# Sixth and seventh product of region (0, 2) in quarters, with measures moved

## The chip, the cores and the metric

The kernel runs on one core of a Trainium2 chip. A core has a matrix engine, TensorE (PE in the profile; PEld is its loading of weights), VectorE (DVE), ScalarE (ACT), GpSimd (POOL) and SyncE (SP). Here POOL and SP mostly issue transfers between HBM and the core's memory. Each engine works through its own queue in order; a wait of one instruction holds up all that stand behind it on the same engine.

The metric is the time of one execution on the device, in microseconds. Before the change it is 1515.66 us, the median of three runs.

## The reference

```python
x = np.matmul(a, b)                       # a, b: 4096 x 4096, float32
return np.where(x > 0, x, alpha * x)      # alpha = 0.01
```

A square matrix product of 4096, and a leaky ReLU on it. The inputs are normally distributed.

## The kernel before, in words

**Arithmetic.** The matmuls run in float16 with sums in float32. The product is formed with Winograd's variant of Strassen's scheme, with 7 products in place of 8, in two levels. The output is cut into 4 x 4 regions of 1024 x 1024, named (g, j) by row group and column group. On the upper level a region takes, for each of two halves of the inner dimension's pairing, blocks A11, A12, A21, A22 and B11, B12, B21, B22; PRODUCTS (L669) lists the seven products:

```python
PRODUCTS = [("a11", 0, 0), ("a12", 1, 0), ("s2", 0, 0), ("s3", 0, 1), ("s1", 0, 0), ("a22", 1, 0), ("s4", 1, 1)]
```

The first is a11 B11, the second a12 B21, and then follow s2 T2, s3 T3, s1 T1, a22 T4 and s4 B22. The letters s are sums of A's blocks, T sums of B's. VectorE makes the T sums in place over the tiles of B: first t3 = B22 - B12, then t2 = B11 + t3, then T4 and T1 (all at the line of b_sum, L606). The sums of A are made once for a row group.

A product as a whole is 64 matmuls of 128 x 512 (L929). It can be done "in quarters", that is with the scheme applied a second time: 7 quarter products of 16 matmuls of 128 x 256 (L773), 112 in all. That needs quarter sums of both operands (sums_of_a, L709 to L728; sums_of_b, L697 to L707), which VectorE makes as well, and additions of the quarter results. Sums of A in quarters are kept in HBM (kept_q) by the first region that makes them, and loaded by those after it.

**Order.** (0, 0) is done within the start, while A and B arrive. Then come (0, 1), (0, 2), (0, 3), then (1, 2), (1, 0), (1, 3), (1, 1), and so on in the four row groups. The order of instructions on each engine is written out by hand (a manual schedule), with no planner: the program's text is the queue of each engine. The flags in_quarters, first_of_group, second_of_group, in_fourth, turning (the last region of a row group) and by_steps (the last region of row group 0) choose the form of each region. Before the change, only regions of row groups 1 to 3 that aren't the last of their group do products in quarters (beside the set FIRST, which does its first product so); row group 0 does all seven as whole products.

**Around a region.** The first product goes to four banks of the accumulator memory, y. ScalarE copies them to the other four, z (L1336), since the second product adds to z, and the third to y. Results leave the accumulators by copies on ScalarE (L952) or additions on VectorE, get the leaky ReLU on VectorE (L328) and are stored by SP (L1258). Tiles of B have two buffers for each of four names. So a tile for the next region can be fetched (POOL at L564, or SP at L561 for halves that have been kept in float16) only when the last product that reads the tile before it is done. In quarters, the first half of a tile comes free earlier or later by the order ks, (0, 1) or (1, 0), in which the two halves are taken.

**T1 in parts.** Where the fourth and fifth products are in quarters, T1's second half is made in four steps of half a tile's columns (L1445): two that make T4 and two that make T1. They stand on VectorE behind the T sums, the leaky ReLU of u1 and two whole sums.

**Measures.** The kernel measures the magnitude of its inputs, to be able to say at its end that float16 with sums of sums was accurate, or else take another path. A measure of a block of A or B is four squares on ScalarE (L235), three additions and a fold on VectorE (L244 to L290). MeasureInTwo does with two buffers, so its third and fourth square (L263) each wait for an addition (L261). Tables say which block is measured in which region and at which place: EARLY begins it ahead of the region's first product and ends it right behind it or, for some, after the T sums ("afterwards"); MEASURED has those in the middle and later; IN_C is a region whose measure takes its room from the buffers of the outputs. A measure has to read a tile of B before a sum overwrites it.

In (0, 3), the squares, the four copies to z and t3 are interleaved (by_steps):

```python
if by_steps:
    for k in ks:
        b_sum(B(0, 1, k), B(1, 1, k), B(0, 1, k), SUB)
        if k == ks[0]:
            next(ends_of_early)
for m in [] if by_steps else at_once:
    m.end()
if not in_first:
    for mt in range(MT):
        nc.scalar.copy(z[mt], y[mt])
```

Of the kernel before, what the change touches and what calls it, by code (L numbers as in the profile page):

```python
# [31 lines left out]
MT = 4  # L32
# [19 lines left out]
def kernel(  # L52
# [167 lines left out]
    class Measure:  # L220
# [21 lines left out]
        def end(self):  # L242
            total, *more = self.held[:3]
            nc.vector.tensor_add(total, total, more[0])  # L244
            if len(self.held) == 3:
                self.square(3)
            nc.vector.tensor_add(total, total, more[1])
            nc.vector.tensor_add(total, total, self.held[3])
            fold(self.which, total, self.place(2), self.pairs)

    class MeasureInTwo(Measure):
# [15 lines left out]

        def end(self):
            for _ in self.parts_of_end():
                pass  # L270
# [206 lines left out]
    for i in range(1, len(steps) - last_turn):  # L477
        t, h, u, first, last = steps[i]
        head = 0 if not new[i] else KC // 2 if last else KC
        groups = [([(mt, c) for c in range(head) for mt in range(MT)], None)]  # L480
        if i == 4:

            groups[0][0].sort(key=lambda x: (x[1] // 2, x[0] == MT - 1))
        if i == 1:
            head = KC // RUNS[u]
            groups = [([(mt, c) for mt in range(MT) for c in range(head)], None)]
        groups += [([(mt, c) for c in range(head, KC)], mt if last else None) for mt in range(MT)]
        following = turns[i + 1] if i + 1 < len(steps) else []
        where = [0, 3] if len(following) < 4 else range(4)
        if i > 1 and i + 1 < len(steps):  # L490
            for fetch in fetches[i + 1]:
                fetch()
        if i == 5:

            for u, nt in ((u, nt) for u in range(2) for nt in range(2)):
                for c in range(0, KC, 4):
                    load_b(1, u, c, 4, nt)
        t, h, u, first, last = steps[i]
        if first:
            banks = {(mt, nt): new_bank(2 * mt + nt) for mt in range(MT) for nt in range(2)}  # L500
            if h not in part:
                part[h] = x_pool.tile([P, MT, 2 * NT], FP32, name="part", tag="x")
        for g, (todo, leaves) in enumerate(groups):
            for mt, c in todo:
                for nt in range(2):
                    mm(banks[mt, nt], h, u, mt, nt, c, first and c == 0, last and c == KC - 1)
            if i == 5 and 1 < g < MT:
                spill(t, h, leaves, banks)
            for piece, turn in enumerate(following):
                if where[piece] == g:  # L510
                    turn()
            if leaves is not None and (i != 5 or g == 1):
                spill(t, h, leaves, banks)
            if leaves is not None and t and i != 5:
                leave_first(h, leaves)
        if i == 3:
            for m in first_columns:
                m.begin()
        if i == 4:
            for m in first_columns:  # L520
                m.end()
            q = quarters_of_first(0)
            f = lambda n: t_of_b21[n].rearrange("p (c n) -> p c n", n=HALF)
            nc.vector.tensor_tensor(f(3), q[1, 1], q[0, 1], SUB)
            nc.vector.tensor_tensor(f(2), f(3), q[0, 0], ADD)
            nc.vector.tensor_tensor(f(4), q[1, 0], f(2), SUB)
# [104 lines left out]
    def judge(line):  # L631
# [26 lines left out]
    A11, A12, A22 = (0, 0, 0), (0, 0, 1), (0, 1, 1)  # L658
# [50 lines left out]
    def sums_of_a(g, name, room, ahead_of_4=None, some=(1, 2, 3, 4), made=None):  # L709
# [5 lines left out]
        def make(n, x0, x1, op):  # L715
# [5 lines left out]
            nc.sync.dma_start(kept_q[name][n - 1], made[n])  # L721
# [162 lines left out]
    for i, (g, j) in enumerate(regions):  # L884

        ks = (1, 0) if in_quarters else (0, 1)
        late_s2 = in_quarters
# [169 lines left out]
        def sixth_in_quarters(pairs, banks, v_pairs, v, y, tq, sq):  # L1057
# [17 lines left out]

            quarter_product(x[0, 0], b[0, 0], into(chain), True)
# [30 lines left out]
        def seventh_in_quarters(y, one, other, tq, sq, between):  # L1107
# [10 lines left out]
            quarter_product(sx(4), b[1, 1], onto(y, 0, 1))  # L1118
# [13 lines left out]
            next(between)  # L1132
            add_pieces(pairs, y)
# [126 lines left out]
        if i == 0:  # L1260
# [6 lines left out]
            first_measure = Measure(0, halves(at[0, 1, 0]) + halves(at[0, 1, 1]), True)  # L1267
# [37 lines left out]
        early = [measure(i, *block, Measure if g else MeasureInTwo) for block in EARLY.get((g, j), [])]  # L1305
        have_t2 = g > KEPT_T.get(j, G)
        by_steps = turning and not g
        at_once, afterwards = ([], early) if in_first or have_t2 else (early[:1], early[1:])
        if by_steps:
            ends_of_early = at_once[0].parts_of_end()  # L1310
# [12 lines left out]
        if (g, j) == LATE:  # L1323
            fetch_b(i, [(1, 1)], ks)
        if second_of_group:
            sums_of_s3(g, (2,))
        if by_steps:
            for k in ks:
                b_sum(B(0, 1, k), B(1, 1, k), B(0, 1, k), SUB)
                if k == ks[0]:  # L1330
                    next(ends_of_early)
        for m in [] if by_steps else at_once:
            m.end()
        if not in_first:
            for mt in range(MT):
                nc.scalar.copy(z[mt], y[mt])  # L1336
        if have_t2:
# [3 lines left out]
        in_c = (g, j) == IN_C  # L1341
        if in_c:
            m = measure(i, *B22)
            m.room = [c_pool.tile([P, 2048], BF16, name="sq", tag=f"c{n}") for n in (side, side, 1 - side, 1 - side)]
            for n in range(4):
                m.square(n)
        if second_of_group:
# [8 lines left out]
        if by_steps:  # L1356
            for k in ks:
                next(ends_of_early)
                b_sum(B(0, 0, k), B(0, 1, k), B(0, 0, k), ADD)
            next(ends_of_early)  # L1360
        for k in [] if by_steps else ks:
            if have_t2:
                if late_s2:
                    load_s2(g, ks[1], True)
                break
            b_sum(B(0, 1, k), B(1, 1, k), B(0, 1, k), SUB)
            if late_s2 and k == ks[0]:
                load_s2(g, ks[1], True)
            b_sum(B(0, 0, k), B(0, 1, k), B(0, 0, k), ADD)
            if g == KEPT_T.get(j):  # L1370
                move_t("t3", j, B(0, 1, k), k, True)
                move_t("t2", j, B(0, 0, k), k, True)
        if middle:
            middle.end()
        if i == 0:
            first_measure.end()
# [10 lines left out]
        if first_of_group:  # L1387
            sum_a(g, "s3")
            if g:
                sum_a(g, "s4")  # L1390
        bring_a(0, 0, range(1 if g else 4))
# [28 lines left out]
        if not g:  # L1420
            bring_a(0, 1, range(3))
# [5 lines left out]
        if g:  # L1427
# [23 lines left out]
        if not g:  # L1451
            bring_a(0, 1, [3])
# [4 lines left out]
        if in_quarters and first_of_group:  # L1457
# [3 lines left out]
            keep_x21(g, "a22")  # L1461
# [63 lines left out]
        if in_quarters and first_of_group:  # L1525
# [4 lines left out]
        if turning:  # L1530
# [7 lines left out]
            fetch_a(1, 0, 3)  # L1538
            load_x21(g, "a22")
# [4 lines left out]
        if in_quarters and first_of_group:  # L1544
# [51 lines left out]
        if in_quarters:  # L1596
# [6 lines left out]
            else:  # L1603
# [5 lines left out]
                if not next_first:  # L1609
                    new_s(g, "s2")  # L1610
                    load_s2(g, 1)
# [84 lines left out]
```

## Time and profile before

| what | value |
|---|---|
| runs | 1512.47, 1515.66, 1516.9 us; median 1515.66 |
| the profiled execution | 1513.17 us, of which the span is 1511.4 |
| granted clock of TensorE | 0.999 |
| start of (0, 1), (0, 2), (0, 3), (1, 2) | 119.74, 216.4, 313.1, 409.8 us |
| start of (1, 0), (1, 3), (2, 3) | 503.34, 593.7, 960.8 us |
| data moved | 385 MB, mean 255 GB/s |

All times within the trace are microseconds from the start of the span. A row of the timeline reads: start, length, engine, line of the code, operation, output and input tiles, their shapes, how many such instructions in a row, and, in brackets, the idle time of the engine just before with what ended it. A row of the chain of work that ended last reads: start, length, what. A row of the engine's waits reads: total, number of times, longest. A line "DMA to landing" gives the shortest, middle and longest time from the issue of a transfer to its landing, for the transfers issued in the window asked for.

### The profile page before, as it was taken

What the parts mean: (1) busy time and instruction counts of PE and PEld (TensorE: products, weight loads), DVE (VectorE), ACT (ScalarE), POOL (GpSimd) and SP (SyncE); (2) the same over time, 40 slices, a digit from 0 to 9 for tenths busy, and PEclk for the clock granted to TensorE, in tenths of its full rate; (3) what the DMA queues carried; (4) which work ended last, traced back from release to release, by engine and by line L of the source; (5) the groups of instructions that cost most, each with busy time, mean ns of one, the idle gap of its engine ahead of it and who ended that gap; (6) DMA issues with size and microseconds to landing.
All of it is one profiled execution on the core that took longest, in us unless ns stands there. A gap on an engine that the chain in (4) does not pass through costs nothing.

```text
span 1511.4 us, 24987 instructions
## 1 busy us (share of the span) xinstructions
PE 1501.6 (99%) x10155; PEld 990.1 (66%) x10155; DVE 1222.6 (81%) x1265; ACT 530.3 (35%) x915; POOL 249.3 (16%) x414
## 2 busy tenths in 40 slices
PE   8999999999999999999999999999999999999998
PEld 3465444444445578884544788887554488888887
DVE  4599866787796799788769698987887888998797
ACT  2402535666510322126561122323574113242322
POOL 5641110224202001013220101000331000100000
PEclk9999999999999999999999999999999999999999
DMA  9999895998989999799898989979989697986845
GB/s 240 189 187 249 232 278 186 152 198 200 272 352 231 287 311 276 271 281 275 207 245 323 292 321 247 357 231 330 232 219 293 256 279 279 254 291 185 348 151 183
DMA packets 192147, 385.00 MB, mean 255 GB/s; under 512 B 17555, under 2 KB 124309, under 8 KB 176662
## 3 DMA queue, kind: packets, MB, share of 16 engines
q0 software_dynamic: 113472, 105.93, 44.1%
q1 hardware_dynamic: 71350, 247.63, 43.6%
q10 hardware_dynamic: 7200, 29.76, 5.1%
q8 instruction: 81, 1.33, 0.3%
q14 instruction: 44, 0.36, 0.1%
HBM read 357.57 MB, written 129.50 MB: 322 GB/s over the span
## 4 chain that ended last, share of the span: by engine, by line
PE 93%; DMA 3%; DVE 1%; POOL 1%; issue 0%; ACT 0%; SPq 0%; DVEq 0%
PE ps L929 47%; PE ps L773 35%; PE ps L910 11%; DMA b<-in_b_dram 2%; PE ps L298 1%; DMA a<-in_a_dram 1%; DVE a L145 0%; POOL b L196 0%; POOL a L136 0%; DMA a_in<-in_a_dram 0%; DVE part L339 0%; DVE a L392 0%; DVE c L1211 0%; PE turned L385 0%; DVE c L328 0%
## 5 line engine op out<-in xcount | busy, mean ns | idle before, releaser
L929 PE MATMUL ps<-b,a 128*128 128x512 f16 x1856 | 403.9, 379 | 0.0
L929 PEld LDWEIGHTS <-a 128*128 128x128 f16 x1856 | 181.3, 98 | 218.4
L929 PE MATMUL ps<-b,s 128*128 128x512 f16 x1408 | 307.5, 379 | 0.0
L929 PEld LDWEIGHTS <-s 128*128 128x128 f16 x1408 | 137.5, 98 | 165.9
L773 PEld LDWEIGHTS <-q 128*128 128x128 f16 x2256 | 220.0, 98 | 27.0 <-issue 0.4
L564 POOL DMA_DIRECT2D b<-in_b_dram x116 | 85.9, 746 | 846.5 <-PE ps L773 338.6
L606 DVE TENSOR_TENSOR b<-b 128x4096 f16<-128x4096 f16 x82 | 185.7, 2287 | 42.1 <-DMA b<-in_b_dram 17.7
L136 POOL DMA_DIRECT2D a<-in_a_dram x252 | 137.5, 552 | 253.3 <-ACT junk L623 80.0
L145 DVE STREAM_TRANSPOSE a<-a 128x512 uint32<-128x512 uint32 (+2 forms) x120 | 126.9, 1107 | 62.6 <-DMA a<-in_a_dram 62.6
L952 ACT COPY c<-ps 128x512 f32<-128x512 f32 x164 | 86.3, 594 | 259.8 <-PE ps L929 139.6
L773 PEld LDWEIGHTS <-a 128*128 128x128 f16 x1584 | 154.7, 98 | 19.5
L328 DVE SCALAR_TENSOR_TENSOR c<-c 128x1024 f32<-128x1024 f32 (+2 forms) x123 | 142.1, 1196 | 5.8 <-ACT c L952 5.6
L623 ACT ACTIVATE junk<-a 128x512 bf16<-128x512 f16 x192 | 121.2, 631 | 68.9 <-DMA a<-in_a_dram 63.7
L235 ACT ACTIVATE sq<-b 128x2048 bf16<-128x2048 f16 x58 | 107.8, 1910 | 67.6 <-DVE sq L244 54.9
L773 PE MATMUL ps<-b,q 128*128 128x256 f16 x1104 | 130.0, 273 | 0.0
L773 PE MATMUL ps<-q,q 128*128 128x256 f16 x1056 | 122.8, 273 | 0.0
L773 PE MATMUL ps<-b,a 128*128 128x256 f16 x1008 | 118.4, 273 | 0.0
L773 PEld LDWEIGHTS <-s 128*128 128x128 f16 x960 | 93.8, 98 | 11.4
L298 PE MATMUL ps<-b,a 128*128 128x512 f16 x384 | 84.9, 379 | 2.0 <-DVE a L392 0.7
L910 PE MATMUL ps<-b,s 128*128 128x256 f16 x768 | 84.8, 273 | 0.0
L910 PE MATMUL ps<-b,a 128*128 128x256 f16 x768 | 84.8, 273 | 0.0
L910 PEld LDWEIGHTS <-s 128*128 128x128 f16 x768 | 75.0, 98 | 8.8
(168 smaller groups left out, 1410.8 us busy)
## 6 DMA issues: line engine op xcount, KB each, us to landing
b<-in_b_dram POOLq DMA_DIRECT2D x124, 512.0 KB, 13.0
out_dram<-c SPq DMA_DIRECT2D x118, 512.0 KB, 8.8
a<-in_a_dram POOLq DMA_DIRECT2D x244, 128.0 KB, 6.4
b<-kept_half SPq DMA_DIRECT2D x30, 1024.0 KB, 11.6
b<-kept SPq DMA_DIRECT2D x20, 1024.0 KB, 10.6
q<-kept_qs ACTq DMA_DIRECT2D x40, 512.0 KB, 7.4
s<-kept_s SPq DMA_DIRECT2D x18, 1024.0 KB, 7.2
q<-kept_qs SPq DMA_DIRECT2D x28, 512.0 KB, 7.0
```

Of the source, the lines that this page charges most:

```text
L136: nc.gpsimd.dma_start(a16[32 * q:32 * q + 32], src.rearrange("(g i) w -> i g w", i=32))
L145: nc.vector.transpose(part.rearrange("p c m e -> p c (m e)").bitcast(U32) .rearrange("p c (g i) -> p g c i", i=32), src[:, :, i * n:(i + 1 ...
L235: nc.scalar.activation(to, self.parts[n], SQUARE)
L298: nc.tensor.matmul(ps, a_cols(at[0, h, u], c, mt), bt[0, u, nt][:, c, :], start=first, stop=last,)
L328: nc.vector.scalar_tensor_tensor(t, t, alpha, t, op0=MULT, op1=MAX if alpha <= 1 else MIN)
L564: nc.gpsimd.dma_start(t[:, c:c + 4, :], b_rows(j, u, c, 4, nt, g > 0))
L606: nc.vector.tensor_tensor(f(to), f(x0), f(x1), op)
L623: nc.scalar.activation(junk, piece[:, q, :], SQUARE, accum_out=to[:, 4 * n + q:4 * n + q + 1])
L773: nc.tensor.matmul(to[m], xq[:, c // 2, rows, c % 2], yq[:, c, :], start=first and c == 0 and m < banks, stop=c == KC - 1, skip_group_chec ...
L910: nc.tensor.matmul(to, a_cols(operand(g, name, k), c, q // 2 * 2 + m), B(half, nt, k)[:, c, q % 2 * HALF:(q % 2 + 1) * HALF], start=False, ...
L929: nc.tensor.matmul(banks[mt], a_cols(t, c, mt), B(half, nt, k)[:, c, :], start=first and (k, c) == todo[0], stop=(k, c) == todo[-1], skip_ ...
L952: nc.scalar.copy(to, bank)
```

## The change

In region (0, 2) the sixth and seventh product (a22 T4 and s4 B22) are done in quarters, as those of (1, 2), (2, 2) and (3, 2) already were. To have the room and the engines' time, these are changed with it:

- (0, 2) makes the quarter sums of a22 and of s4 itself, with no storing of them; s4's are made between the quarter products (made_here), and the last of its quarter products is put at the end.
- The measure of A21 goes from (0, 1) into the start, (0, 1) measures A11 instead, A12 is measured early in (0, 2), and A22 in (0, 3) after the fourth product, in the room of the next s2. So (0, 2) no longer holds measures of A22, A11, B12 and A12 at its later places.
- B21 of the last column group is measured in (1, 3) rather than in (2, 3); (2, 3) measures B12, in the room of outputs, ahead of the sum t3 that overwrites it.
- The quarter sums of (0, 2) take the buffer that held s2 of row group 0, which (0, 1) had made for all regions of the group; (0, 3) makes its s2 again, with two sums on VectorE, behind its T sums.
- (0, 2) fetches the next region's B22 in the order (1, 0) of halves, and (0, 3) takes its halves in that order.
- In (1, 0) the copies to z are put ahead of the fourth square, and VectorE's order there is: t3 of one half, first addition of the measure, t2 of that half, the rest of the measure, four quarter sums of s1, t3 and t2 of the other half. Before: measure, quarter sums, four T sums.
- In (1, 3) the fetch of B22 is issued ahead of the first product, and so ahead of the load of s2 on SP's queue.

```diff
+        if i == 1:
+            m = Measure(0, halves(at[0, 1, 0]) + halves(at[0, 1, 1]), True, c_rooms)
+            for n in range(4):
+                m.square(n)
+            m.end()
...
     EARLY = {
-        (0, 3): [B11], (1, 0): [B21], (1, 1): [B11], (2, 3): [B21], (2, 1): [B12], (3, 1): [B21],
+        (0, 2): [A12], (0, 3): [B11], (1, 0): [B21], (1, 3): [B21], (1, 1): [B11], (2, 1): [B12], (3, 1): [B21],
     }
-    IN_C = (3, 0)
+    IN_C = {(2, 3): B12, (3, 0): B22}
     MEASURED = {
-        (0, 1): (None, [B22], B12, B11), (0, 2): (B21, [B22, A22, A11], B12, A12),
+        (0, 1): (None, [B22], B12, B11), (0, 2): (B21, [B22], None, None),
...
-        late_s2 = in_quarters
+        late_s2 = in_quarters and g > 0
...
+            def made_here(n, room=None):
+                next_s[n] = new_a16() if room is None else room
+                f = lambda t: by_chunk(next_s[t]) if isinstance(t, int) else x4[t]
+                x0, x1, op = {1: ((1, 0), (1, 1), ADD), 2: (1, (0, 0), SUB),
+                              3: ((0, 0), (1, 0), SUB), 4: ((0, 1), 2, SUB)}[n]
+                nc.vector.tensor_tensor(f(n), f(x0), f(x1), op)
+
+            if g == 0:
+                quarter_product(x[0, 0], b[0, 0], into(chain), True)
+                nc.scalar.copy(one, chain)
...
+                made_here(1)
+                next_t[4] = tq[2]
+                sums_of_b(y7, next_t, (4,))
+                quarter_product(sx(3), b[0, 1], into(chain))
+                nc.scalar.copy(one, chain)
+                more(1, 1, chain)
+                made_here(2)
+                quarter_product(sx(4), b[1, 1], into(other))
+                more(0, 1, other)
+                quarter_product(x[1, 1], t(4), into(one))
+                more(1, 0, one)
+                next_t[1] = tq[4]
+                sums_of_b(y7, next_t, (1,))
+                made_here(3)
+                made_here(4, sq["room"])
+                return next_t, next_s
...
+            if g == 0:
+                quarter_product(sx(4), b[1, 1], onto(y, 0, 1))
...
-        in_quarters = g > 0 and not turning
-        in_fourth = in_quarters and not first_of_group
+        in_quarters = not turning and (g > 0 or i > 0)
+        six_seven = in_quarters and (first_of_group or not g)
+        in_fourth = in_quarters and not six_seven
...
+        copies_first = bool(at_once) and second_of_group
+        if by_steps or copies_first:
+            ends_of_early = at_once[0].parts_of_end()
...
+        if (g, j) == LATE:
+            fetch_b(i, [(1, 1)], ks)
...
         if by_steps:
-            for k in ks:
-                b_sum(B(0, 1, k), B(1, 1, k), B(0, 1, k), SUB)
-                if k == ks[0]:
-                    next(ends_of_early)
-        for m in [] if by_steps else at_once:
+            t3_sum(ks[0])
+            next(ends_of_early)
+        for m in [] if by_steps or copies_first else at_once:
             m.end()
         if not in_first:
             for mt in range(MT):
                 nc.scalar.copy(z[mt], y[mt])
+        if copies_first:
+            t3_sum(ks[0])
+            next(ends_of_early)
+            t2_sum(ks[0])
+            for _ in ends_of_early:
+                pass
...
+            for k in ks:
+                a_sum(s[g, "s2", k], s[g, "s1", k], at[g, 0, k], SUB)
...
+            for k in ks[1:] if copies_first else ks:
+                t3_sum(k)
+                if in_c and not have_t2 and k == ks[1]:
+                    for _ in range(3):
+                        next(ends_in_c)
+                t2_sum(k)
+            if in_c and not have_t2:
+                next(ends_in_c)
...
+            if by_steps:
+                m = measure(i, *A22, MeasureInTwo)
+                m.room = [t.bitcast(BF16) for t in halves(whole_s[g + 1, "s2"][:, 0])]
+                m.begin()
+                m.end()
```

More of the change, by code (lines that the diff above doesn't have):

```diff
@@ L1346 @@
                 m.square(n)
+            if not second_of_group:
+                ends_in_c = m.parts_of_end()
         if second_of_group:
@@ L1375 @@
         if i == 0:
-            first_measure.end()
+            ends_of_first = first_measure.parts_of_end()
+            next(ends_of_first)
         for m in [] if have_t2 else afterwards:
@@ L1388 @@
             sum_a(g, "s3")
+            for _ in ends_of_first if not g else ():
+                pass
             if g:
                 sum_a(g, "s4")
-        bring_a(0, 0, range(1 if g else 4))
+        bring_a(0, 0, range(1 if g else 2))
+        if by_steps:
+            next(ends_of_early)
+            bring_a(0, 0, range(2, MT))
         product(1, z, False)
```

93 lines of the change are left out of this document (57 added, 36 removed).

## The prediction

> **What bounds the kernel now.** I read the engines' share of the span first, then the waits of the matmul engine, then the chain that ended last.
>
> ```profile
> PE 1501.6 (99%) x10155; PEld 990.1 (66%) x10155; DVE 1222.6 (81%) x1265; ACT 530.3 (35%) x915; POOL 249.3 (16%) x414
> ```
> ```profile
> PE turned L385 <- DVE a_rounded L369: 1.3, 1, 1.3
> ```
> ```profile
> 119.74 359.15 PE ps L929 x1664
> ...
> 544.78 61.19 PE ps L773 x560
> ...
> 633.91 48.95 PE ps L773 x448
> ...
> 724.30 12.23 PE ps L773 x112
> 736.53 110.51 PE ps L929 x512
> ...
> 1000.99 48.91 PE ps L773 x448
> ```
>
> The matmul engine works for 1501.6 us of the span of 1511.4, and its longest single wait in the whole program is 1.3 us, during the start. From 119.74 on the chain is nothing but matmuls, piece against piece. So a matmul less is time less, in full; and a wait that appears anywhere after 119.74 has no slack in front of it and is paid in full. That makes the question of this change a plain one: what matmuls it saves, against where VectorE (81% busy, and the supplier of every sum) now comes late.
>
> The chain also gives the prices. 110.51 / 512 = 215.8 ns per matmul of 512 columns, 12.23 / 112 = 109.2 ns per matmul of 256.
>
> **The change part by part.** *The two products of (0, 2).* A whole product is 64 x 215.8 ns = 13.81 us; in quarters it is 112 x 109.2 = 12.23. Two of them save 2 x 1.58 = 3.16 us. This is the only saving on the matmul engine, so it is the ceiling of the gain: 0.21% of the time.
>
> [...]
>
> *What is free.* The measure of A21 in the start (4 squares, 5 or so VectorE rows, about 8 + 7 us) falls where both engines have nothing to do:
>
> ```profile
> 47.72 0.58 ACT L337 COPY part<-ps 128x512 f32<-128x512 f32 x1 [21.84 <-PE ps L298]
> ```
> ```profile
> 48.51 2.04 DVE L145 STREAM_TRANSPOSE a<-a 128x1024 uint32<-128x1024 uint32 x1 [10.73 <-DMA a<-in_a_dram]
> ```
> ```profile
> 216.40:313.10 96.70, 96.70 (x450) 43.75 (x448) 66.36 (x75) 53.98 (x45) 11.87 (x16) 1.00 0.86 184
> 313.10:409.80 96.70, 96.70 (x450) 43.76 (x448) 73.86 (x83) 60.79 (x146) 35.88 (x66) 1.00 0.97 218
> ```
>
> Those are idle stretches of 21.8 us on ScalarE and 10.7 us on VectorE; cost 0, and if the last tile of A21 landed later, up to about 2 us. In the windows of (0, 2) and (0, 3) the busy times of PE, PEld, VectorE, ScalarE and POOL stand behind the length: VectorE has 66.4 and 73.9 of 96.7 us. The quarter sums of (0, 2) (4 for a22, 4 for s4, the T sums at 1.2 us each) replace two measures there, and A22's measure (about 10 us) plus the two sums of s2 (2.3 us each) go into the 22.8 us left in (0, 3). I take 0 for all of these, 0 to 1 us as bounds. POOL and SP issue as many transfers as before; in (1, 0) SP's second load of s2 goes a little earlier, behind the first t3, and costs nothing.
>
> *(0, 3), the copies to the second set of banks.* Its fetch of B22 now follows the order of the quarters, and its first half can only be fetched once the next-to-last quarter product of (0, 2) has released the tile, about 308.2 us (counted with the 2.8 us saved by then), not 306.75.
>
> ```profile
> 306.75 0.75 POOL L564 DMA_DIRECT2D b<-in_b_dram  x1 [5.42 <-ACT sq L235]
> 307.89 0.74 POOL L564 DMA_DIRECT2D b<-in_b_dram  x1 [0.40 <-issue]
> ```
> ```profile
> DMA to landing us min/median/max: 7.9/9.8/11.7
> ```
> ```profile
> DMA to landing us min/median/max: 8.9/11.2/13.6
> ```
> ```profile
> 319.69 2.29 DVE L606 TENSOR_TENSOR b<-b 128x4096 f16<-128x4096 f16 x1
> 322.50 1.23 DVE L261 TENSOR_TENSOR sq<-sq 128x2048 bf16<-128x2048 bf16 x1 [0.51 <-ACT sq L235]
> ```
> ```profile
> 323.76 1.91 ACT L263 ACTIVATE sq<-b 128x2048 bf16<-128x2048 f16 x1 [1.29 <-DVE sq L261]
> 325.57 2.03 ACT L1336 COPY ps<-ps 128x512 f32<-128x512 f32 x4
> ```
>
> The five fences are POOL's rows, the landing times of these two fetches and of the next two, VectorE's and ScalarE's rows. ScalarE's queue holds: third square, then the four copies that the second product accumulates on. The square waits for VectorE's first add, that for the first t3 sum, that for B22. So the first copy ends at landing + 2.3 + 1.2 + 1.9 + 0.5 = landing + about 6.1 (0.2 of it hand-overs). The second half leaves POOL near 309.4 instead of 307.89. The second product starts at 313.10 + 13.81 - 3.16 = 323.8. With the latency of 11 us, between the medians of both pairs and the upper row, landing is 320.4 and the wait 320.4 + 6.1 - 323.8 = 2.7 us; with 7.9 it is 0, with 13.6 it is 5.3. I take 2.7, nearest to the half that it replaces.
>
> *(1, 0), the T sums.* The order on VectorE is now: t3 of one half, first add, t2 of that half, adds and fold of the measure, four quarter sums of s1, t3 and t2 of the other half. Before, measure and quarter sums stood ahead of all T sums.
>
> ```profile
> 496.65 1.48 POOL L564 DMA_DIRECT2D b<-in_b_dram  x2 [5.51 <-PE ps L773]
> ```
> ```profile
> DMA to landing us min/median/max: 21.8/22.7/23.6
> ```
> ```profile
> 510.39 1.22 DVE L244 TENSOR_TENSOR sq<-sq 128x2048 bf16<-128x2048 bf16 x1
> ...
> 517.29 0.69 DVE L275 TENSOR_TENSOR sq<-sq 128x1024 bf16<-128x1024 bf16 x1
> ...
> 519.94 1.22 DVE L720 TENSOR_TENSOR q<-s 128x2048 f16<-128x2048 f16 x1
> ...
> 524.60 2.29 DVE L606 TENSOR_TENSOR b<-b 128x4096 f16<-128x4096 f16 x1
> ...
> 533.72 2.35 DVE L328 SCALAR_TENSOR_TENSOR c<-c 128x1024 f32<-128x1024 f32 x2
> ```
> ```profile
> 530.80 13.98 PE L929 MATMUL ps<-b,s 128*128 128x512 f16 x64
> ```
>
> The half of B22 for the first t3 leaves POOL at 496.65 and 497.4 and lands 21.8 and 23.6 us later, at 521.0. Before, VectorE used the time from 510.39 to 524.60 for the measure and the quarter sums. After, t3 stands first, and VectorE is idle from 510.4 until 521.0. From there: t3 523.3, add 524.5, t2 526.9, two adds and a fold of 519.94 - 517.29 = 2.65 to 532.1, four quarter sums to 537.0, t3 539.3, t2 541.6. The third product starts at 530.80 with the half whose t2 is done, and needs the other half after 32 matmuls, at 537.9: a wait of 3.7 us. Behind it the leaky pair (2.35), two sums for T4 and T1 (4.6) and three quarter parts of T1 (1.18 each) end at 552.0. The fifth product, which was at 544.78 and is now at 548.5, needs the third part in its second quarter, 1.75 us later at 550.2: 1.8 us more. Together 5.5. Lower end 0, if the fetch takes under 18.5 us; upper end 8, if it takes 2.5 us more.
>
> *(1, 3), the measure ahead of u1.* Measuring B21 here puts ten VectorE rows between the four T sums and the leaky pair; in (1, 1) the same rows ran from 688.78 to 695.88, 7.1 us. Against it the load of B22 is now ahead of that of s2 on SP's queue.
>
> ```profile
> 604.25 0.34 SPq L792 DMA_DIRECT2D s<-kept_s  x1
> 604.64 0.91 SPq L561 DMA_DIRECT2D b<-kept_half  x2
> ```
> ```profile
> DMA to landing us min/median/max: 9.2/10.2/11.2
> ```
> ```profile
> 613.96 2.29 DVE L606 TENSOR_TENSOR b<-b 128x4096 f16<-128x4096 f16 x1 [9.00 <-DMA b<-kept_half]
> ...
> 627.14 4.69 DVE L606 TENSOR_TENSOR b<-b 128x4096 f16<-128x4096 f16 x2 [1.77 <-DMA kept_half<-b]
> 631.75 4.62 DVE L1445 TENSOR_TENSOR b<-b 128x2048 f16<-128x2048 f16 x4
> ```
> ```profile
> 688.78 1.22 DVE L244 TENSOR_TENSOR sq<-sq 128x2048 bf16<-128x2048 bf16 x1
> ...
> 695.88 2.29 DVE L606 TENSOR_TENSOR b<-b 128x4096 f16<-128x4096 f16 x1
> ```
>
> One megabyte ahead less is worth 2 to 4 us (the two halves of B22 landed 2.4 us apart); I take 3.0, landing 610.9. So the chain shifts by 7.1 - 3.0 - 1.8 (the idle time before 627.14) = 2.3 us. The third of the four parts at 631.75 ends at 635.2, and the second quarter of the fifth product, at 633.91 + 1.75, needs it at 635.7: slack 0.45. Wait 2.0 us, with bounds 0.3 and 3.
>
> *(2, 3), B12 measured ahead of t3.* t3 overwrites B12 in place, and so now stands behind the squares of it.
>
> ```profile
> 971.94 2.28 DVE L606 TENSOR_TENSOR b<-b 128x4096 f16<-128x4096 f16 x1
> ```
> ```profile
> 973.61 5.51 ACT L235 ACTIVATE sq<-b 128x2048 bf16<-128x2048 f16 x3
> ```
>
> Squares start on ScalarE at 973.61 and take 1.84 each, so two are done at 977.4 and four at 981.0. The first t3 starts at 977.4, not 971.94; t2 ends at 982.0; then t3, three adds, t2 and fold to 992.9, leaky 995.2, two sums 999.8, three parts and one t3 quarter to 1004.6. The second quarter of the fifth product is due at 1000.99 + 1.75 = 1002.7: a wait of 1.9 us, between 0 (the measure that stood there before is gone too) and 4.
>
> Sum: -3.16 + 2.7 + 5.5 + 2.0 + 1.9 = +8.9 us. The profiled execution took 1513.17 (span 1511.4), which gives 1522.1. It lies 2.5 us under the median of the runs, 1515.66, which gives 1524.6. I predict 1523, between the two. A difference below about 0.3%, 4.5 us, can hardly be told from no change here.
>
> **The rivals.** *B22 lands early in (1, 0).* A single mechanism on the other side: the price of 5.5 hangs on a landing at 521.0. If it lands 5.1 us sooner, at 515.9 or before, t2 is done by 536.5, nothing waits there, and the sum is +3.4: 1516.6 on the profile's basis, not measurably slower. For it: other fetches took 8 to 14 us. Against it: this one took 21.8 and 23.6, and what is queued ahead of it is unchanged. It decides with the others as given. Chance 0.17.
>
> *All covers hold.* VectorE comes late nowhere, and only the matmuls count: 1513.2 - 3.2 = 1510.0 to, with the median, 1512.5. For it: each wait above is 2 to 6 us, and landing times vary by as much. Against it: four places would have to be wrong together, and two of them hang on no transfer. Chance 0.18.
>
> *The clock falls in a wait.* Its place is the wait of 3.7 us in (1, 0); nothing of the kind exists in before, whose longest wait is 1.3 us (granted clock 1.00, the third number from the right, in both windows quoted). If matmuls ran at half speed behind it for 8 to 32 matmuls, each 215.8 ns more, it costs 1.7 to 6.9 us: about 1525. It decides when a wait is long enough to trigger it, which no run here shows. [...] Chance 0.08.
>
> **How the numbers follow.** The forecast, waits in at least three of the four places, has 0.57; its own range is 1516 to 1530. Of it 0.05 ends within 0.3% after all. Slower: 0.52 + 0.08 = 0.60. Within: 0.05 + 0.17 + 0.14 = 0.36. Faster by over 0.3% needs more than the ceiling of 3.16 us, thus chance between runs: 0.04 of the second rival. The range starts at 1511, inside that rival, and ends at 1530: all upper ends together (5.3 + 8 + 3 + 4 - 3.16 = 17.1) give 1530.3 on the profile's basis.
>
> **What would show it.** Right: 224 more matmuls of 256 columns in (0, 2) and the chain of matmuls broken at four places, each released by VectorE or ScalarE: copies of the second product in (0, 3), t2 in (1, 0) at the third product's middle, parts of T1 in (1, 3) and (2, 3); VectorE idle for about 10 us in (1, 0) ahead of the first t3. Wrong: no wait of the matmul engine above 1.3 us, or waits at other places, such as the last quarter of (0, 2), where s4's sums are made late, or (1, 2), which inherits VectorE's backlog of (0, 3).

## The result, and the profile after

The changed kernel takes 1533.31 us (median of five runs, 1528.5 to 1534.16), the one before 1516.9 on the same chip: a ratio of 1.0106, with a 95% interval from 1.0089 to 1.0123. The profiled execution has a span of 1526.6 us, 15.2 more than the 1511.4 of before. The direction was forecast, but the time lies above the range, which ended at 1530. The profile is of the shortest of the five runs, 1528.5 us; the others took 1530.35 to 1534.16, and no trace shows what they lost beyond the rows below.

The matmul engine's timeline of the changed kernel, with only those of its rows after the start that have a wait in brackets (start, length, line, operation, shapes, count, idle time before and what ended it):

```profile
436.01 13.97 PE L939 MATMUL ps<-b,s 128*128 128x512 f16 x64 [1.33 <-DVE b L615]
...
464.78 13.99 PE L939 MATMUL ps<-b,s 128*128 128x512 f16 x64 [0.98 <-ACT c L962]
...
489.54 1.91 PE L783 MATMUL ps<-q,a 128*128 128x256 f16 x16 [0.29 <-ACT ps L1144]
...
521.66 15.66 PE L939 MATMUL ps<-b,a 128*128 128x512 f16 x64 [4.18 <-ACT ps L1401]
...
547.01 8.62 PE L939 MATMUL ps<-b,s 128*128 128x512 f16 x32 [2.78 <-DVE b L615]
...
645.37 1.92 PE L783 MATMUL ps<-b,s 128*128 128x256 f16 x16 [0.29 <-DVE b L615]
...
648.77 1.91 PE L783 MATMUL ps<-b,s 128*128 128x256 f16 x16 [1.48 <-DVE b L1527]
...
1017.62 1.91 PE L783 MATMUL ps<-b,s 128*128 128x256 f16 x16 [1.40 <-DVE b L1527]
```

Against before, where nothing after 119.74 waited, there are eight waits: three in (1, 2), two in (1, 0), two in (1, 3), one in (2, 3). In (0, 3) no row shows one; only its first 128 matmuls take 28.05 us in place of 27.79. Two rows also show something that is no wait: the 64 matmuls behind the wait of 4.18 take 15.66 us instead of 13.98, and the 32 behind that of 2.78 take 8.62, where the first 32 of the same product took 7.07. The granted clock of the changed kernel in the stretches around these (window, its length, busy us of PE, PEld, VectorE, ScalarE and POOL, granted clock, share of transfers, GB/s) says why:

```profile
521.60:523.60 2.00, 1.94 (x8) 0.88 (x8) 0.00 (x0) 1.47 (x4) 0.00 (x0) 0.82 1.25 207
523.60:525.60 2.00, 2.00 (x7) 0.63 (x6) 0.00 (x0) 0.00 (x0) 0.00 (x0) 0.50 1.24 206
...
547.00:549.00 2.00, 1.99 (x5) 0.69 (x5) 2.00 (x2) 0.00 (x0) 0.00 (x0) 0.50 0.98 397
549.00:551.00 2.00, 2.00 (x8) 0.81 (x7) 2.00 (x2) 0.00 (x0) 0.00 (x0) 0.71 0.98 223
```

The granted clock fell to half around both waits. In stretches of 0.2 us it reads 0.50 from 522.9 to 526.3 and from 546.8 to 550.2, 3.4 us each time.

Where the 15.2 us stand follows from the times at which the same products start. These are the rows of the matmul engine at the start of (0, 3), (1, 2), (1, 0), the second product of (1, 3) and (1, 1), and, from the chain of work, the start of (2, 1), in the changed kernel:

```profile
309.85 28.05 PE L939 MATMUL ps<-b,a 128*128 128x512 f16 x128
...
406.81 27.88 PE L939 MATMUL ps<-b,a 128*128 128x512 f16 x128
...
503.51 13.98 PE L939 MATMUL ps<-b,a 128*128 128x512 f16 x64
...
616.97 14.14 PE L920 MATMUL ps<-b,a 128*128 128x256 f16 x128
...
696.18 27.79 PE L939 MATMUL ps<-b,a 128*128 128x512 f16 x128
```
```profile
1065.19 41.44 PE ps L939 x192
```

and in the kernel before, from (1, 2) on:

```profile
409.65 27.79 PE L929 MATMUL ps<-b,a 128*128 128x512 f16 x128
...
503.17 27.79 PE L929 MATMUL ps<-b,a 128*128 128x512 f16 x128
...
605.80 14.14 PE L910 MATMUL ps<-b,a 128*128 128x256 f16 x128
...
682.70 27.79 PE L929 MATMUL ps<-b,a 128*128 128x512 f16 x128
```
```profile
1049.89 41.44 PE ps L929 x192
```

| stretch | lead of before at its end | lost in it, us | forecast |
|---|---|---|---|
| (0, 2) | -3.1 | -3.2 | -3.16 |
| (0, 3) | -2.8 | 0.3 | 2.7 |
| (1, 2) | 0.3 | 3.2 | 0 |
| (1, 0), and the first product of (1, 3) | 11.2 | 10.8 | 5.5 |
| the rest of (1, 3) | 13.5 | 2.3 | 2.0 |
| to the end of (2, 3) | 15.3 | 1.8 | 1.9 |

((0, 3) started at 312.96 in the timeline of before; the chain of work calls it 313.10, and the row of the product before it ends at 313.13, 0.17 us after that start.) The saving, (1, 3) and (2, 3) came as forecast. (1, 2) and (1, 0) make the difference, and (0, 3) goes the other way.

**(1, 2).** VectorE's timeline of the changed kernel at the end of (0, 3) and in (1, 2):

```profile
378.79 1.23 DVE L269 TENSOR_TENSOR s<-s 128x2048 bf16<-128x2048 bf16 x1 [6.71 <-ACT s L235]
382.00 1.23 DVE L269 TENSOR_TENSOR s<-s 128x2048 bf16<-128x2048 bf16 x1 [1.98 <-ACT s L271]
385.20 1.23 DVE L269 TENSOR_TENSOR s<-s 128x2048 bf16<-128x2048 bf16 x1 [1.98 <-ACT s L271]
...
394.11 6.06 DVE L145 STREAM_TRANSPOSE a<-a 128x512 uint32<-128x512 uint32 x6
...
431.29 9.26 DVE L615 TENSOR_TENSOR b<-b 128x4096 f16<-128x4096 f16 x4 [1.60 <-DMA b<-kept]
```

and of the kernel before:

```profile
386.31 6.06 DVE L145 STREAM_TRANSPOSE a<-a 128x512 uint32<-128x512 uint32 x6
...
422.21 9.27 DVE L606 TENSOR_TENSOR b<-b 128x4096 f16<-128x4096 f16 x4
```

The measure of A22 holds VectorE from 372 to 389.5 with 3.7 us of work in the first 14: its additions alternate with squares on ScalarE, and each waits for the other. The six transposes of the next row group's A stand behind it and come 7.8 us later. POOL's fetches of A wait for the rooms that they free; eight that were issued from 388.95 on in the kernel before now come later:

```profile
396.76 4.30 POOL L136 DMA_DIRECT2D a<-in_a_dram  x8 [14.25 <-DVE a L145]
```

The T sums of (1, 2) start 9.1 us later (some 7.4 by this delay, and 1.6 by a wait for a load, in brackets above), while the matmuls are 2.8 us ahead. So t2 comes 1.33 us late.

**(1, 0).** ScalarE's timeline of the changed kernel:

```profile
511.01 1.91 ACT L235 ACTIVATE sq<-b 128x2048 bf16<-128x2048 f16 x1 [6.23 <-DMA b<-in_b_dram]
515.14 1.91 ACT L235 ACTIVATE sq<-b 128x2048 bf16<-128x2048 f16 x1 [2.22 <-DMA b<-in_b_dram]
519.22 1.91 ACT L235 ACTIVATE sq<-b 128x2048 bf16<-128x2048 f16 x1 [2.17 <-DMA b<-in_b_dram]
521.03 2.04 ACT L1401 COPY ps<-ps 128x512 f32<-128x512 f32 x4
```

Before, the third square ran at 510.70 and the fourth at 514.09. Now the third waits until 519.22 for its quarter of B21, with the copies behind it; and VectorE's first t3 waits until 526.89 for B22, not 521.0. The fetches were issued at nearly the same time (489.55 and 496.98, before 489.66 and 496.65), but took 27 to 31 us to land in place of 21 to 24. What stands beside them is SP's timeline, in the changed kernel:

```profile
457.44 5.43 SPq L731 DMA_DIRECT2D kept_qs<-q  x4
469.09 5.49 SPq L731 DMA_DIRECT2D kept_qa<-q  x4
```

and in the one before:

```profile
448.38 4.30 SPq L721 DMA_DIRECT2D kept_qs<-q  x4
457.90 3.90 SPq L721 DMA_DIRECT2D kept_qa<-q  x4
```

VectorE's delay reaches the quarter sums of (1, 2), so 4 MB of stores move by 9 and 11 us, into the time when B for (1, 0) is fetched (472 to 498). Other transfers of (1, 2) moved with them. That the stores delay the landing is argued from times so far; the experiments test it.

### The profile page after: what moved, and what is told of

Same layout as the page of the kernel before. It is cut to its first block, busy times and chain, and to the rows that moved or that the text cites. A ratio compares the mean times of both kernels' runs of the same rounds, so it can differ in the third digit from the quotient of the medians.

```text
span 1526.6 us, 25216 instructions
## 1 busy us (share of the span) xinstructions
PE 1503.5 (98%) x10251; PEld 1001.8 (66%) x10251; DVE 1251.9 (82%) x1293; ACT 532.1 (35%) x918; POOL 249.9 (16%) x414
## 5 line engine op out<-in xcount | busy, mean ns | idle before, releaser
L939 PE MATMUL ps<-b,a 128*128 128x512 f16 x1792 | 392.0, 380 | 4.3 <-ACT ps L1401 4.2
L939 PEld LDWEIGHTS <-a 128*128 128x128 f16 x1792 | 175.8, 98 | 216.3 <-issue 7.4
L939 PE MATMUL ps<-b,s 128*128 128x512 f16 x1344 | 295.2, 380 | 5.1 <-DVE b L615 4.1
L783 PEld LDWEIGHTS <-q 128*128 128x128 f16 x2384 | 232.8, 98 | 28.8 <-issue 1.4
L939 PEld LDWEIGHTS <-s 128*128 128x128 f16 x1344 | 131.8, 98 | 165.0 <-issue 6.8
L783 PEld LDWEIGHTS <-a 128*128 128x128 f16 x1632 | 159.7, 98 | 20.4 <-issue 0.5
L783 PE MATMUL ps<-b,q 128*128 128x256 f16 x1168 | 137.3, 273 | 0.0
L783 PE MATMUL ps<-q,q 128*128 128x256 f16 x1120 | 130.1, 273 | 0.3
L783 PE MATMUL ps<-b,a 128*128 128x256 f16 x1040 | 122.2, 273 | 0.0
L783 PEld LDWEIGHTS <-s 128*128 128x128 f16 x1008 | 98.5, 98 | 15.6 <-issue 3.2
L302 PE MATMUL ps<-b,a 128*128 128x512 f16 x384 | 84.9, 379 | 2.3 <-DVE a L396 0.7
L920 PE MATMUL ps<-b,a 128*128 128x256 f16 x768 | 84.8, 273 | 0.0
L920 PEld LDWEIGHTS <-a 128*128 128x128 f16 x768 | 75.1, 98 | 8.7
```

The lines of the kernel that those rows point to most:

```text
L302: nc.tensor.matmul(ps, a_cols(at[0, h, u], c, mt), bt[0, u, nt][:, c, :], start=first, stop=last,)
L783: nc.tensor.matmul(to[m], xq[:, c // 2, rows, c % 2], yq[:, c, :], start=first and c == 0 and m < banks, stop=c == KC - 1, skip_group_chec ...
L920: nc.tensor.matmul(to, a_cols(operand(g, name, k), c, q // 2 * 2 + m), B(half, nt, k)[:, c, q % 2 * HALF:(q % 2 + 1) * HALF], start=False, ...
L939: nc.tensor.matmul(banks[mt], a_cols(t, c, mt), B(half, nt, k)[:, c, :], start=first and (k, c) == todo[0], stop=(k, c) == todo[-1], skip_ ...
```

## The experiments

The theory after the result: A22's measure, placed where VectorE waits for its squares, delays the next row group's A, with it the stores of (1, 2), and with these the landing of B in (1, 0); the new order in (1, 0) costs a second wait there; both waits make the clock fall to 0.50. The first rival is that the quartering itself, which sets everything 3 us ahead, makes the backlog of transfers.

**Without A22's measure.**

```diff
             if by_steps:
-                m = measure(i, *A22, MeasureInTwo)
-                ...
-                m.end()
```

> The changed kernel without the measure of A22 in (0, 3); the statistic of A22 is left out. Theory (the measure, whose additions wait on VectorE for squares, holds up the transposes of the next row group, and with them the sums of (1, 2), its stores and so the landing of B in (1, 0)): the waits of 1.3 and 1.0 us in (1, 2) and the 4.2 us for the copies in (1, 0) go, with the slow matmuls behind the latter (1.7 us); the wait for t2 in (1, 0) stays, at 2.8 to 3.7 us. About 1526, 8 us less than the changed kernel. Rival (the backlog of transfers comes from the quarters of (0, 2), which set everything 3 us ahead): the 4.2 us stay, 1530 to 1533.

Measured: 1523.55 us, ratio to before 1.0047 (1.0029 to 1.0065); the kernel before took 1515.76 in these runs. The waits of its matmul engine:

```profile
325.65 13.97 PE L939 MATMUL ps<-b,a 128*128 128x512 f16 x64 [2.25 <-ACT ps L1401]
541.28 9.78 PE L939 MATMUL ps<-b,s 128*128 128x512 f16 x32 [4.54 <-DVE b L615]
641.55 1.92 PE L783 MATMUL ps<-b,s 128*128 128x256 f16 x16 [1.35 <-DVE b L615]
644.95 1.91 PE L783 MATMUL ps<-b,s 128*128 128x256 f16 x16 [1.48 <-DVE b L1527]
1013.77 1.91 PE L783 MATMUL ps<-b,s 128*128 128x256 f16 x16 [1.39 <-DVE b L1527]
```

The three waits of (1, 2) and that for the copies in (1, 0) are gone, as the theory has it: by the medians 9.8 us less than the changed kernel, more than the 8 expected, although a wait of 2.25 appears in (0, 3). The stores of the quarter sums are back at 450.50 and 460.02, and B22 in (1, 0) lands at 521.2. The wait for t2 remains and is 4.54, longer than expected, since the product before it no longer waits.

**The old order in (1, 0).**

```diff
-        copies_first = bool(at_once) and second_of_group
+        copies_first = False
```

> The changed kernel with the order of before in (1, 0): measure, quarter sums of s1, then four T sums; copies behind the fourth square. Theory: t2 is no longer what the third product waits for (2.8 us and 1.7 us of slow matmuls go), but the copies, still held up by the late landing, come some 2 us later: 1530 to 1531. Rival (the order doesn't matter, since B22 lands late in any order): 1533.

Measured: 1527.66, ratio 1.0069 (1.0052 to 1.0085). The second product of (1, 0):

```profile
527.93 16.89 PE L939 MATMUL ps<-b,a 128*128 128x512 f16 x64 [6.75 <-ACT ps L1401]
```

t2 is waited for no more; the copies are now behind the fourth square, and the second product waits 6.75 us, 2.6 more than in the changed kernel, with 2.9 us of slow matmuls. (0, 3) has a wait of 2.91 for the copies, too. The profiled execution took 1530.21, as expected; the median lies 2 to 3 us below, which neither theory explains. The rows show a trade: the new order keeps the copies off the fourth square and pays for it at t2.

**Both.** (The two edits above together.)

> Both edits together; the statistic of A22 is left out. Theory: no wait is left in (1, 2) and (1, 0); what stays are 1.8 us in (1, 3) and 1.4 in (2, 3), against the 3.2 saved, so the time of the kernel before, about 1517. Rival (backlog from the quarters): at least 4 us more, 1521.

Measured: 1520.25, ratio 1.0028 (1.0015 to 1.0041). (1, 2) is free, but 3 us more than expected are left:

```profile
326.49 13.97 PE L939 MATMUL ps<-b,a 128*128 128x512 f16 x64 [2.68 <-ACT ps L1401]
519.74 15.54 PE L939 MATMUL ps<-b,a 128*128 128x512 f16 x64 [2.88 <-ACT ps L1401]
```

One is the wait for the copies in (0, 3) that the prediction had put at 2.7. The other is in (1, 0): the copies wait there even in the old order. The time lies nearer to the rival's 1521 than to the 1517 of the theory, so the measure of A22 isn't the whole cause of late copies in (1, 0).

**The quartering alone.** (No A22, B21 in (1, 3) or B12 in (2, 3) is measured, and the order in (1, 0) is the old one. The other moves of the change stay, among them the measures of A11, A12 and A21 at their new places.)

```diff
-        (0, 2): [A12], (0, 3): [B11], (1, 0): [B21], (1, 3): [B21], ...
+        (0, 2): [A12], (0, 3): [B11], (1, 0): [B21], ...
-    IN_C = {(2, 3): B12, (3, 0): B22}
+    IN_C = {(3, 0): B22}
```

> As the one before, and B21 in (1, 3) and B12 in (2, 3) aren't measured either; three statistics are left out. What is left is the quartering of (0, 2). Theory: all four places are free of waits, 3.2 us below the kernel before: about 1513.5. Rival (the quartering brings waits of its own): 1517 or more.

Measured: 1516.18, ratio 1.0001 (0.999 to 1.0012): the expectation missed, and the rival has a part. The waits of (1, 3) and (2, 3) are gone, so the two measures do cause these. But one of 2.06 us for the copies in (1, 0) is left, 0.17 in (0, 3), and 1.5 between (2, 2) and (2, 0), where a quarter sum on VectorE waits 1.55 us for the matmul engine as it didn't before; why, I haven't followed. Together they take back the 3.2 us. ScalarE's timeline of this kernel in (1, 0):

```profile
509.43 1.91 ACT L235 ACTIVATE sq<-b 128x2048 bf16<-128x2048 f16 x1 [3.14 <-DMA b<-in_b_dram]
514.44 1.91 ACT L235 ACTIVATE sq<-b 128x2048 bf16<-128x2048 f16 x1 [3.10 <-DMA b<-in_b_dram]
516.25 2.03 ACT L1401 COPY ps<-ps 128x512 f32<-128x512 f32 x4
```

The fetches of B21 for these squares were issued 2.3 us earlier than in before (487.34 against 489.66), and the fourth square still waits until 514.44, against 514.09: its fetch took 26.3 us to land, against 23.6. In these two executions transfers set the time: being early at their start moved nothing at their end.

**A22's measure mended, and the rest as in the changed kernel.** The squares go to four rooms and need no addition between them; the additions stand behind the transposes.

```diff
-                m = measure(i, *A22, MeasureInTwo)
-                m.room = [t.bitcast(BF16) for t in halves(whole_s[g + 1, "s2"][:, 0])]
-                m.begin()
-                m.end()
+                m = measure(i, *A22)
+                m.room = [t.bitcast(BF16) for k in range(2) for t in halves(whole_s[g + 1, "s2"][:, k])]
+                for n in range(4):
+                    m.square(n)
+                ends_of_a22 = m.parts_of_end()
...
+        if by_steps:
+            for _ in range(3):
+                next(ends_of_a22)
...
                 add(u2[::-1], z[::-1])
+        if by_steps:
+            next(ends_of_a22)
```

> The changed kernel with one edit: A22's squares in four rooms, its additions behind the transposes. The measure is made. Theory (place and waits of the measure): as without it, 1523 to 1525, with no wait in (1, 2), and in (1, 0) only that of t2. Rival (the extra 6 to 7 us of VectorE): 1530 to 1533, with the copies in (1, 0) waiting about 4 us.

Measured: 1522.48, ratio 1.0047 (1.0032 to 1.0062), before at 1515.82. It is the same ratio as without the measure. There is no wait in (1, 2), and in (1, 0) only that for t2:

```profile
538.98 8.64 PE L939 MATMUL ps<-b,s 128*128 128x512 f16 x32 [4.54 <-DVE b L615]
```

So the measure's work costs nothing that can be told from the noise (the interval is some 2 us to either side); its place and its back and forth with ScalarE cost the 9 us by the ratios, or 10.8 by the medians. Which of the two counts for more wasn't tried apart.

**All mends together**, with every measure made: the one above, the old order in (1, 0), and in (0, 3) the copies ahead of the third square.

```diff
         if by_steps:
+            for mt in range(MT):
+                nc.scalar.copy(z[mt], y[mt])
             t3_sum(ks[0])
             next(ends_of_early)
...
-        if not in_first:
+        if not in_first and not by_steps:
```

> The whole change with three mends, and all measures made: in (0, 3) the four copies stand ahead of the third square; in (1, 0) the order of before; the squares of A22 go to four rooms, so that they wait for nothing on VectorE, and their additions stand behind the transposes of the fifth product's time. Theory: no wait in (0, 3) and (1, 2), one of 2 to 3 us for the copies in (1, 0), where the landing of B21 sets the time, 1.3 and 1.4 us in (1, 3) and (2, 3): about 1.5 to 3 us over the kernel before, 1517 to 1519. Rival (it is the extra work of the measure on VectorE, not its place and waits): (1, 2) and (1, 0) wait as in the changed kernel, 1525 or more.

Measured: 1518.82, ratio 1.0018 (1.0005 to 1.0032), 3.0 us over before. The waits left are 1.48 for the copies in (1, 0), where 2 to 3 were expected, 1.20 in (1, 3) and 1.39 in (2, 3), as expected, and a new one of 1.02 in (0, 3). There ScalarE's copies of the second product's result stand behind its reading of the next row group's A, which waits 8.4 us for a transfer; whether the mend in (0, 3) brought this about isn't known. No version that was run beats the kernel before.

**A pause by itself, in the kernel before.** To see the clock without the change, VectorE repeats a reduction of 0.69 us in (1, 0), 8 times.

```diff
+            for _ in range(again[0]):
+                nc.vector.tensor_reduce(...)     # the one above once more
...
+        again[0] = 8 if (g, j) == (1, 0) else 0
```

> The kernel before, with the 0.69 us reduction at the end of B21's measure in (1, 0) done 8 times more, which changes no value: 5.5 us of VectorE, of which 1.6 is slack ahead of the third product. Theory (a wait of the matmul engine above some 2.7 us is followed by slow matmuls): a wait of 3.9 us at the third product, and its 64 matmuls take 1.4 to 2.9 us more than 13.98; 5.3 to 6.8 us over before. Rival (slow matmuls have another cause in the changed kernel, such as its transfers): 13.98 behind the wait, 3.9 us over before.

Measured: 1522.02, ratio 1.0031 (1.0018 to 1.0044), by the medians 6.2 us over before. The timeline row of the third product, and the clock behind the wait:

```profile
538.37 16.82 PE L935 MATMUL ps<-b,s 128*128 128x512 f16 x64 [4.59 <-DVE b L612]
```
```profile
538.40:540.40 2.00, 2.00 (x5) 0.67 (x5) 2.00 (x1) 0.00 (x0) 0.00 (x0) 0.50 0.99 283
540.40:542.40 2.00, 2.00 (x6) 0.73 (x5) 1.97 (x2) 0.00 (x0) 0.00 (x0) 0.50 0.94 295
```

A wait of 4.59 cost 4.59 + 2.84. (This execution also waited 1.64 for the copies of the second product, whose 64 matmuls then took 13.97.) So in this run a wait of 4.59 by itself, without the change, was followed by a granted clock of 0.50 and slow matmuls, 16.82 us for the 64 in place of 13.98.

**A shorter pause**, 5 times.

> The same with 5 repeats: 3.45 us of VectorE, a wait of 1.9 us. Theory: no slow matmuls, 13.98 behind the wait, 1.9 us over before. Rival (any wait slows the matmuls behind it, in proportion): about 0.7 us more.

Measured: 1517.74, ratio 1.0006 (0.9994 to 1.0019), by the medians 1.9 us over before, as expected, though the interval holds no change as well. The row decides: the third product waited 1.78 us, and its 64 matmuls then took the usual 13.97:

```profile
531.92 13.97 PE L935 MATMUL ps<-b,s 128*128 128x512 f16 x64 [1.78 <-DVE b L612]
```

**More stores, in the kernel before.** SP stores 2 MB more in (1, 2), behind the stores of the quarter sums.

```diff
+    twice = dram_pool.tile([2, P, KC * RM], DT, name="twice")
...
             keep_x21(g, "a22")
+            if g == 1:
+                for k in range(2):
+                    nc.sync.dma_start(twice[k], at[g, 0, k].rearrange("p c m e -> p (c m e)"))
```

> The kernel before with 2 MB more of stores: in (1, 2), behind the stores of quarter sums that end at 462, SP stores two tiles of A that nothing reads. VectorE's and ScalarE's orders are as before. Theory (late stores, which share the transfer engines with the fetches of B for (1, 0), are what makes these land late): the B21 squares in (1, 0) come 3 to 7 us later, and the copies to the second banks make the second product wait 2 to 5 us, with slow matmuls if it is over 2.7: 2 to 7 us over before. Rival (the fetches land late because of VectorE or of their own issue): landing as before, no wait, the time of before.

Measured: 1523.63, ratio 1.0040 (1.0024 to 1.0056), before at 1516.47. SP issues them at 464.42. The only wait of the run after the start is in (1, 0). These are the fourth square of B21 on ScalarE and, behind it and the copies, the second product:

```profile
523.18 1.91 ACT L235 ACTIVATE sq<-b 128x2048 bf16<-128x2048 f16 x1 [0.69 <-DMA b<-in_b_dram]
```
```profile
525.63 16.85 PE L930 MATMUL ps<-b,a 128*128 128x512 f16 x64 [7.29 <-ACT ps L1337]
```

The fourth square runs at 523.18 rather than 514.09, 9 us later. Of these, 1.2 us are that this execution issues the fetches later; its fetch took 31.5 us to land in place of 23.6. An estimate of the size: before, transfers ran at a mean of 252 GB/s from 455 to 520, and 2.1 MB more take 8.3 us at that rate. So late stores alone, with the orders of VectorE and ScalarE untouched, are enough for the late landing and the wait in (1, 0). The wait was longer than the 2 to 5 us expected. What the other transfers that moved in the changed kernel add wasn't tried apart.

## Why the prediction was wrong in size

*The saving* of 3.16 us was right: (0, 2) takes 3.17 us less. The prices from the chain held: in the changed kernel the 224 matmuls of 256 in (0, 2) take 24.45 us, 109.2 ns each, and a whole product of (0, 2) 13.82.

*"What is free"* is the step that failed first. It counted A22's measure as "about 10 us" of VectorE's idle time in (0, 3), "0 to 1 us as bounds". The idle time was there, but in an ordered queue idle time has a place: the measure stood ahead of six transposes that POOL's fetches wait for. It cost 3.2 us in (1, 2), and by way of the stores the wait for the copies in (1, 0), 4.18 and 1.7 of slow matmuls. The prediction itself named (1, 2), "which inherits VectorE's backlog of (0, 3)", as a sign of being wrong, and still put its price at nothing. Without the measure, and with it mended, the kernel is by the medians 9.8 and 10.8 us faster. The profiled executions are only 4.0 and 7.6 us shorter, since the wait for t2 in (1, 0) grows as that for the copies goes, and without the measure (0, 3) waits too; the rest lies between executions, and no trace shows it.

*(1, 0)* was put at 5.5, with a landing at 521.0, because "what is queued ahead of it is unchanged". In order it was; in time it wasn't, as 4 MB of stores had moved into it. The copies waited 4.18, which no step had. B22 took 29.1 us to land, 5.5 more than before, where the upper end of 8 us allowed 2.5. The order of VectorE was read rightly: it was idle until B22 landed (16 us, forecast 10.6), and t2's second half came 2.78 late (forecast 3.7). That these two are near is in part luck, since VectorE's sums and the third product were both some 6 us later than forecast; with the landing back at 521.2, t2 came 4.54 late. The wait of 1.8 for the third part of T1 didn't come, since the slow matmuls behind t2 gave VectorE 1.5 us.

*The clock* was a rival at a chance of 0.08 for (1, 0); it happened, twice, at 1.7 and 1.5 us; in the experiments the loss was 1.4 to 2.9 us. That the matmuls would run at half speed, and 8 to 32 of them, was my assumption, and no run had shown it by then. The changed kernel's rows show a granted clock of 0.50 for 3.4 us around each of the two waits, and a loss of 1.4 to 2.9 us is 215.8 ns more for some 6 to 13 matmuls.

*(0, 3)* was right in its mechanism, and its size depends on the landing: t3 starts when B22 lands, at 318.0 in the changed kernel's profile (no wait), 318.6 and 317.4 with the quartering alone and with A22's measure mended (0.17 and 0.30), and 319.8, 320.3 and 320.6 in the first three experiments, with waits of 2.25, 2.91 and 2.68. The forecast had 320.4 and 2.7.

*(1, 3) and (2, 3)* were right: 1.8 and 1.4 of waits against 2.0 and 1.9 (the terms for (1, 3), 2.3 less a slack of 0.45, give 1.85), and gone when the two measures are left out. The steps hold as well: less the 11.2 and 13.5 us by which the matmuls are late there, B22 lands in (1, 3) at 610.9 and the first t3 of (2, 3) starts at 977.4, both as forecast.

*The rivals.* "All covers hold" and "B22 lands early in (1, 0)" both fell. The range's upper end summed the upper bounds of the steps that I had, and had no room for a step that I had put at nothing.

## What to carry to other kernels

A measure's idle engine time is no room by itself: before work is placed in an in-order queue, ask which instructions stand behind it, whom they release, and whether it will sit there waiting for another engine; the same work, with rooms enough and placed some rows later, cost nothing that the runs could tell (a ratio of 1.0047 with it and without). In (1, 0), where the fourth square waited for its transfer, a lead of 2.3 us at the issue was gone at the landing (514.44 against 514.09; the quartering alone gave nothing). With 2 MB more of stores issued ahead of it, 1.78 us on SP, the fetch for that square took 31.5 us to land in place of 23.6. And each single wait of the matmul engine of 2.78 us or more cost 1.4 to 2.9 us beyond its length here.

## What the runs showed of the hardware

In all profiles here, each wait of the matmul engine of 2.78 us and more, after the start, was followed by slow matmuls: 1.5 us lost behind 2.78, 1.6 behind 2.88, 1.4 behind 2.91, 1.7 behind 4.18, 2.7 and 1.6 behind two of 4.54, 2.8 behind 4.59, 2.9 behind 6.75 and 7.29. No wait of up to 2.68 was, among them 2.06, 2.25 and 2.68. (Behind one of 1.02 in the kernel with all mends a product took 14.79 us, 0.8 more, but at a granted clock of 1.00 from 350.8 to 366.6; why, I haven't followed.) Whether it is the length of the wait that decides, and from where on, so few waits can't show.

What is lost doesn't follow the length of the wait. In the changed kernel, read in stretches of 0.2 us, the granted clock falls 5.4 and 2.5 us after the matmuls stop, the first time 1.2 us after they have begun again, and stands at 0.50 for 3.4 us both times; 3.4 and 3.2 of these lie behind the wait, and the losses of 1.7 and 1.5 us are near half of that. In the kernel before with the pause of 4.59 it stands at 0.50 for the first 4.0 us behind the wait and at a mean of 0.66 for the next 2.6, and 2.8 are lost. Two waits of 4.54 cost 2.7 and 1.6 us: without A22's measure the clock still reads 0.50 from 3.4 us after the matmuls begin again, and with it mended 1.00. These are the stretches from 3.4 to 5.4 us behind the two waits, the first without the measure, the second with it mended:

```profile
544.70:546.70 2.00, 2.00 (x6) 0.69 (x5) 1.90 (x2) 0.00 (x0) 0.00 (x0) 0.50 0.90 317
```
```profile
542.40:544.40 2.00, 2.00 (x11) 0.88 (x9) 1.90 (x2) 0.00 (x0) 0.00 (x0) 1.00 0.88 320
```

The waits measured are of the matmuls' stream as the profile models it.

Fetches of B by POOL, 512 KB each, landed 8 to 14 us after their issue in (0, 3) of the kernel before and 21 to 24 us for those issued from 489 to 498 in (1, 2), with the same share of transfers in both stretches (1.15 from 300 to 330 and from 485 to 522). Those of the latter place took 27 to 31 us in the changed kernel and 28 to 32 with 2 MB more of stores, which were enough for a wait of 7.29 us.
